# Sigmoid-gated halves of 8192 x 8192: 64 neighbouring rows for each partition

## The chip, the core and the metric

The kernel runs on one core of one Trainium2 chip. The core has compute engines that run side by side: ScalarE (ACT) for functions such as the sigmoid, VectorE (DVE) for elementwise arithmetic, and others that this kernel leaves idle. Data comes from the chip's main memory (HBM, "dram" in names) to the on-chip memory of 128 partitions by DMA transfers. Sixteen DMA engines carry them. A transfer is issued by an engine's queue: here SyncE (SP) issues the loads, ScalarE the stores.

The metric is the device time of a run in microseconds (us).

## The reference

The input x has 8192 rows of 8192 float32 numbers. The left half of each row is multiplied by the sigmoid of the right half:

```python
def reference(x):                       # x: (8192, 8192) float32
    a, b = np.split(x, 2, axis=-1)      # two halves of 4096 columns
    return a * (1 / (1 + np.exp(-b)))   # (8192, 4096) float32
```

The kernel must read 268.4 MB and write 134.2 MB. Each element is used once.

## The kernel before

The rows are cut into 32 tiles of 256 rows. A tile puts two rows on each of the 128 partitions, so a partition holds 2 x 8192 x 4 B = 64 KiB of a tile of x, and 32 KiB of a tile of the result. There are two buffers for x and two for the result, used in turn.

```python
    R = 2
    SLOTS = 2
    n_tiles = n_rows // (P * R)                              # 8192 / 256 = 32
    x_t = x.rearrange("(n p r) m -> n p (r m)", p=P, r=R)    # row = n*256 + p*2 + r
    out_t = out.rearrange("(n p r) m -> n p (r m)", p=P, r=R)

    xs = [pool.tile([P, R * n_cols], fp32, name=f"x_sb{k}") for k in range(SLOTS)]
    os = [pool.tile([P, R * half], fp32, name=f"o_sb{k}") for k in range(SLOTS)]
    ... # (cut)
    for i in range(n_tiles):
        rows = xs[i % SLOTS].rearrange("p (r h m) -> p r h m", r=R, h=2)
        packed = os[i % SLOTS].rearrange("p (r m) -> p r m", r=R)

        load = nc.sync.dma_start(out=xs[i % SLOTS], in_=x_t[i])      # L50
        ... # (cut: waits)
        if 0 < i < n_tiles - 1:
            parts = [(slice(0, R), slice(0, half))]          # one part: the whole tile
        else:
            ... # (cut: first and last tile in four parts)
        def store(cols):
            ins = nc.scalar.dma_start(out=out_t[i, :, cols], in_=os[i % SLOTS][:, cols])   # L62
            ... # (cut)
        for k, (r, c) in enumerate(parts):
            b = rows[:, r, 1, c]
            sig = nc.scalar.activation(out=b, in_=b, func=SIG)                             # L68
            mul = nc.vector.tensor_mul(out=packed[:, r, c], in0=rows[:, r, 0, c], in1=b)   # L69
            ... # (cut: waits; the last tile stores each part)
        store(chunks[-1] if i == n_tiles - 1 else slice(0, R * half))
```

Line numbers after # are those that the profile gives. `x_t[i]` is tile i of the rearranged input: for each partition p it names one run of memory. The load into a buffer waits until the multiply has read the tile that was there. The code that is cut declares which waits are needed, issues the first load early and orders the end of the program.

Of the kernel before, what the change touches and what calls it, by code (L numbers as in the profile page):

```python
# [1 line left out]

# [4 lines left out]


def _tiles(ctx, tc, x, out):

    nc = tc.nc
    P = nc.NUM_PARTITIONS  # L20
    DEP = mybir.DependencyInfo(mybir.DependencyClass.Sync, mybir.DependencyReason.DATA)
    fp32 = mybir.dt.float32
    SIG = mybir.ActivationFunctionType.Sigmoid

    n_rows, n_cols = x.shape
    half = n_cols // 2
    R = 2
    SLOTS = 2
    n_tiles = n_rows // (P * R)
    x_t = x.rearrange("(n p r) m -> n p (r m)", p=P, r=R)  # L30
    out_t = out.rearrange("(n p r) m -> n p (r m)", p=P, r=R)

    pool = ctx.enter_context(tc.tile_pool(name="io", bufs=1))
    xs = [pool.tile([P, R * n_cols], fp32, name=f"x_sb{k}") for k in range(SLOTS)]
    os = [pool.tile([P, R * half], fp32, name=f"o_sb{k}") for k in range(SLOTS)]

    def implied(later, *earlier):
        for e in earlier:
            tc.declare_no_dep(later.ins, e.ins, reason="follows from the waits that are kept")

    gone = [{k: [] for k in ("loads", "sigs", "muls", "stores")} for _ in range(SLOTS)]
    last_stores = [[] for _ in range(SLOTS)]
    for i in range(n_tiles):
        old = gone[i % SLOTS]
        freed = last_stores[i % SLOTS]
        now = {k: [] for k in old}
# [4 lines that stand above are left out]
        implied(load, *old["loads"], *old["sigs"])  # L51
        now["loads"].append(load)

        if 0 < i < n_tiles - 1:
            parts = [(slice(0, R), slice(0, half))]
        else:
            w = half // 2
            parts = [
                (slice(r, r + 1), slice(c * w, (c + 1) * w)) for r in range(R) for c in range(2)
            ]  # L60
        def store(cols):
            ins = nc.scalar.dma_start(out=out_t[i, :, cols], in_=os[i % SLOTS][:, cols])  # L62
            now["stores"].append(ins)

        chunks = []
# [4 lines that stand above are left out]
            implied(sig, *old["sigs"], *old["muls"], *old["loads"])  # L70
            implied(mul, *old["muls"], *old["loads"], *now["loads"])
            by_sigmoid = i % 2 == 1 and len(parts) == 1
            implied(mul, *(s for s in old["stores"] if by_sigmoid or s not in freed))
            if by_sigmoid:
                for s in freed:
                    tc.add_manual_dep(sig.ins, s.ins.name, DEP, reason="frees the output slot")
            tc.keep_in_program_order(sig)
            now["sigs"].append(sig)
            now["muls"].append(mul)
            chunks.append(slice(r.start * half + c.start, r.start * half + c.stop))  # L80
            if i == n_tiles - 1 and k > 0:
                store(chunks[k - 1])
        store(chunks[-1] if i == n_tiles - 1 else slice(0, R * half))
        for s in now["stores"]:
            implied(s, *old["loads"], *old["sigs"], *old["muls"], *now["loads"], *now["sigs"])
        for k in old:
            old[k] += now[k]
        last_stores[i % SLOTS] = now["stores"]


def _launch_early(nc):

    SP = mybir.EngineType.SP
    entry, body = (b.instructions for b in nc.main_func.blocks[:2])
    load = next(i for i in body if i.engine == SP and i.opcode == "DMACopy")
    assert not load.sync_info.on_wait
    body.remove(load)
    where = next(k for k, i in enumerate(entry) if i.engine == SP and i.opcode == "Drain")  # L100
    entry.insert(where, load)


def _close_on_sync(nc):

    SP, POOL = mybir.EngineType.SP, mybir.EngineType.Pool  # L110
    ACT = mybir.EngineType.Activation
    block = nc.main_func.blocks[2].instructions
    waits = block[0]
    assert waits.engine == SP and waits.opcode == "Drain" and len(waits.sync_info.on_wait) > 1
    pool = [i for i in block if i.engine == POOL]
    drain1, gather1, release1, reset, clear, drain2, gather2, release2 = pool
    assert reset.is_reset_sema and clear.opcode == "ISA"
    others = [i for i in block[1:] if i.engine != POOL]
    arrive = [i for i in others[: len(others) // 2] if i.opcode == "Drain"]
    assert len(arrive) == 4  # L120
    body = nc.main_func.blocks[1].instructions
    last = [i for i in body if i.engine == ACT and i.opcode == "DMACopy"][-1].sync_info.on_update[0].id
    final = [w for w in waits.sync_info.on_wait if w.id == last]
    assert len(final) == 1

    def event(engine, wait, update=()):
        return mybir.InstEventSemaphore(
            name=nc.get_next_instruction_name(),
            engine=engine,
            debug=waits.debug,  # L130
            sync_info=mybir.SyncInfo(on_wait=[wait], on_update=list(update)),
        )

    n = len(block)
    for lo, hi in ((reset.reset_range_start, last), (last + 1, reset.reset_range_stop)):
        if lo < hi:
            nc.gpsimd.sem_clear(range(lo, hi))
    clears = block[n:]
    assert clears and all(i.opcode == "ISA" for i in clears)
    back = mybir.SyncUpdate(  # L140
        sync_type="semaphore",
        id=last,
        ant_name=final[0].ant_name,
        update_mode="sem-sub-imm",
        update_value=final[0].wait_value,
        update_reg=None,
    )
    block[:] = [
        *arrive,
        drain1,  # L150
        gather1,
        *(event(POOL, w) for w in waits.sync_info.on_wait if w.id != last),
        reset,
        *clears,
        drain2,
        event(SP, final[0], [back]),
    ]


@with_exitstack  # L160
def kernel(
    ctx: ExitStack,
    tc: tile.TileContext,
    x: bass.AP,
    out: bass.AP,
):
    nc = tc.nc
    with ExitStack() as pools:
        _tiles(pools, tc, x, out)
    tc.close()  # L170
    tc.compile()
    _launch_early(nc)
    _close_on_sync(nc)


# [1 line left out]
_INS = ['x']  # L177
_OUTS = [((8192, 4096), 'float32')]


# [23 lines left out]
```

## Time and profile before

| What | Before |
|---|---|
| Time, median of 3 runs | 933.17 us (933.12 to 933.89) |
| Span of the profiled run | 931.7 us |
| VectorE busy | 278.7 us in 38 multiplies |
| ScalarE busy | 227.1 us, 225.8 of it in 38 sigmoids |
| Read from HBM, written to HBM | 268.44 MB, 134.22 MB |
| Mean rate of all transfers | 432 GB/s |
| Load of one tile, issue to landing (median) | 42.2 us |
| Store of one whole tile, issue to landing (median) | 34.7 us |

"Busy" is the time in which an engine executes an instruction; idle time of an engine that is not the bottleneck costs nothing. For the DMA engines the profile gives the mean busy share of the 16 and the bytes that they moved. A transfer is cut into packets, and the profile counts these, their bytes and their time for each queue: q1 carries the loads, q10 the stores. "Issue to landing" has in it the time in which a transfer stands in its queue behind others. The chain of waits goes back from the last instruction of the run, each time to what released it.

### The profile page before, as it was taken

To read this page: it belongs to the slowest core of one execution; us is meant where nothing else is said; L and a number is where in the kernel's file an instruction comes from. 1 tells how busy PE (TensorE), PEld (TensorE's weight loads), DVE (VectorE), ACT (ScalarE), POOL (GpSimd) and SP (SyncE) were. 2 spreads that over 40 slices of the span, in tenths; PEclk is the share of its full clock that TensorE was granted. 3 is DMA by queue.
4 is the path that set the end of the run, shared out by engine and by line. 5 is a ranking of instruction groups with operands and counts; after the bars stand their busy time and mean duration, and the time that the engine had idled before them with its cause. 6 is when DMAs were issued, how large, how long until landed. Compare 5 with 4: busy or idle time off the path is not lost.

```text
span 931.7 us, 247 instructions
## 1 busy us (share of the span) xinstructions
DVE 278.7 (30%) x38; ACT 227.1 (24%) x39; POOL 0.2 (0%) x4
## 2 busy tenths in 40 slices
DVE  0333213333133331233312333123331233312333
ACT  1323330233311333113331133311333113332033
POOL 0000000000000000000000000000000000000000
DMA  9999999999999999999999999999999999999999
GB/s 405 428 450 428 422 456 405 450 428 428 450 418 438 428 436 442 428 428 450 447 408 428 442 459 428 413 460 411 450 428 425 453 408 447 428 428 450 425 430 405
DMA packets 9649, 402.67 MB, mean 432 GB/s; under 512 B 1072, under 2 KB 1072, under 8 KB 1072
## 3 DMA queue, kind: packets, MB, share of 16 engines
q1 hardware_dynamic: 4608, 268.44, 66.6%
q10 hardware_dynamic: 5040, 134.22, 33.4%
q14 instruction: 1, 0.01, 0.0%
HBM read 268.44 MB, written 134.22 MB: 432 GB/s over the span
## 4 chain that ended last, share of the span: by engine, by line
DMA 73%; DVE 15%; ACT 12%; issue 0%; ACTq 0%
DMA x_sb<-in_x_dram 73%; DVE o_sb L69 15%; ACT x_sb L68 12%; ACTq L62 0%; ACTq L68 0%
## 5 line engine op out<-in xcount | busy, mean ns | idle before, releaser
L69 DVE TENSOR_TENSOR o_sb<-x_sb 128x8192 f32<-128x8192 f32 (+1 forms) x38 | 278.7, 7344 | 647.1 <-ACT x_sb L68 647.1
L68 ACT ACTIVATE x_sb<-x_sb 128x8192 f32<-128x8192 f32 (+1 forms) x38 | 225.8, 5952 | 695.6 <-DMA x_sb<-in_x_dram 694.4
L68 ACT ACT_TABLE_LOAD x1 | 1.3, 1283 | 0.8 <-PEq L188 0.8
L188 POOL MEMSET const-bfloat16-1.0<- 128x1 bf16 x1 | 0.1, 102 | 0.0
L188 POOL MEMSET const-uint8-127<- 128x1 uint8 x1 | 0.1, 102 | 0.0
L188 POOL MEMSET const-float32-0.0<- 128x1 f32 x1 | 0.1, 99 | 0.2 <-issue 0.2
L188 POOL MEMSET const-float32-1.0<- 128x1 f32 x1 | 0.1, 99 | 0.0
## 6 DMA issues: line engine op xcount, KB each, us to landing
out_dram<-o_sb ACTq DMA_DIRECT2D x31, 4096.0 KB, 34.7
out_dram<-o_sb ACTq DMA_DIRECT2D x4, 1024.0 KB, 5.6
x_sb<-in_x_dram SPq DMA_DIRECT2D x32, 42.2
```

Of the source, the lines that this page charges most:

```text
L68: sig = nc.scalar.activation(out=b, in_=b, func=SIG)
L69: mul = nc.vector.tensor_mul(out=packed[:, r, c], in0=rows[:, r, 0, c], in1=b)
L188: nc = _bacc.Bacc("TRN2", target_bir_lowering=False, num_devices=1)
```

## The change

The rows are given to partitions in another order. Before, tile n is a block of 256 neighbouring rows, of which partition p takes rows 2p and 2p+1. After, partition p takes rows 64p to 64p+63 over the whole run, two for each tile: tile n has rows 64p + 2n and 64p + 2n + 1 for every p. Each row is still handled once, and the result of a row goes to the same place in the output as before, as the output is rearranged in the same way. The change is meant to let each partition walk through one region of memory from the first tile to the last.

```diff
@@ -27,8 +27,8 @@
     R = 2
     SLOTS = 2
     n_tiles = n_rows // (P * R)
-    x_t = x.rearrange("(n p r) m -> n p (r m)", p=P, r=R)
-    out_t = out.rearrange("(n p r) m -> n p (r m)", p=P, r=R)
+    x_t = x.rearrange("(p n r) m -> n p (r m)", p=P, r=R)
+    out_t = out.rearrange("(p n r) m -> n p (r m)", p=P, r=R)
```

This is the whole diff. From one partition to the next, a tile of x now steps 64 rows (2 MiB) in memory instead of 2 rows (64 KiB), and a tile of the output 64 rows of 16 KiB (1 MiB) instead of 32 KiB.

## The prediction

> **What bounds the kernel now.** I read the share of busy time first, then the slices, the DMA queues, the chain, the groups by form, and one table of windows. The share of busy time says which engines cannot be the bound:
>
> ```profile
> DVE 278.7 (30%) x38; ACT 227.1 (24%) x39; POOL 0.2 (0%) x4
> ...
> DMA  9999999999999999999999999999999999999999
> ...
> DMA packets 9649, 402.67 MB, mean 432 GB/s; under 512 B 1072, under 2 KB 1072, under 8 KB 1072
> ```
>
> VectorE works 30% of the span, ScalarE 24%, and the 16 DMA engines are at nine tenths or more in all 40 slices. So the transfers bound the kernel. A finer look, at whole periods of two tiles, removes the rounding:
>
> ```profile
> 100.00:158.00 58.00, 17.39 (x2) 14.06 (x2) 0.00 (x0) 1.00 1.00 434
> 390.00:448.00 58.00, 17.38 (x2) 14.06 (x2) 0.00 (x0) 1.00 1.00 434
> 738.00:796.00 58.00, 17.39 (x2) 14.06 (x2) 0.00 (x0) 1.00 1.00 434
> ```
>
> The columns are the stretch and its length, then VectorE, ScalarE and GpSimd busy, the clock, the DMA share and GB/s. Early, in the middle and late, the share is 1.00 and the rate 434 GB/s: there is no gap in which a transfer waits for an engine. The queues split that time:
>
> ```profile
> q1 hardware_dynamic: 4608, 268.44, 66.6%
> q10 hardware_dynamic: 5040, 134.22, 33.4%
> ```
>
> q1 is the loads (268.44 MB = 8192 x 8192 x 4 B), q10 the stores. 268.44 MB in 66.6% of 16 x 931.7 us is 27.0 GB/s for one DMA engine, and 134.22 MB in 33.4% is 27.0 GB/s too: a load and a store cost the same per byte now. The counts of packets tell their sizes: 32 loads x 128 partitions = 4096 pieces of 64 KiB, plus 32 x 16 = 512 small ones, is 4608. The small ones I take to be the completion signals (one for each engine and transfer: 67 transfers x 16 = 1072, as the page counts under 512 B).
>
> ```profile
> L69 DVE TENSOR_TENSOR o_sb<-x_sb 128x8192 f32<-128x8192 f32 x30 | 260.8, 8692 | 608.1 <-ACT x_sb L68 608.1
> L68 ACT ACTIVATE x_sb<-x_sb 128x8192 f32<-128x8192 f32 x30 | 210.9, 7031 | 652.8 <-DMA x_sb<-in_x_dram 652.8
> ...
> DMA x_sb<-in_x_dram 73%; DVE o_sb L69 15%; ACT x_sb L68 12%; ACTq L62 0%; ACTq L68 0%
> ```
>
> The chain gives 27% to ScalarE and VectorE, which looks like a gain to be had there. It isn't: the chain goes through one buffer slot, 42 us of load, 7.03 of sigmoid and 8.69 of multiply, and while the 15.7 us of compute run, the other slot's load and a store hold the DMA engines full, as the 1.00 says. ScalarE idles 652.8 us, all of it for loads.
>
> **What the skill says.** Three places of the Trainium skill bear on this.
> - DMA: Bandwidth & Descriptors, "Where 436 GB/s comes from": the 16 ports of the on-chip memory carry 435.2 GB/s. The trace agrees: 434 measured.
> - HBM Reference, "Specifications (TRN2)": a pair of cores shares about 716 GB/s. If so, memory now has room to spare, and some loss there could stay hidden. No view of this trace shows a memory limit.
> - DMA: Bandwidth & Descriptors, "Latency and other measured facts", the row on row pitch at large powers of two: memory-to-memory copies of 128 partitions x 16 KiB ran at 214 GB/s per direction when the pitch from partition to partition was padded, at 207 with a pitch of 512 KiB, at 164 with 2 MiB, and at 103 with 4 or 8 MiB; the page calls aliasing of memory channels among partitions that run in step an inference. The trace of the kernel before is at a pitch of 64 KiB and is at full rate; it neither shows nor refutes the row.
>
> **The change part by part.** Only two address patterns change.
> - *Engines and waits:* nothing. The order of instructions on each engine is the same: 34 rows on VectorE, 71 on ScalarE, 34 on SyncE in both. The 38 sigmoids and 38 multiplies keep their shapes, so 278.7 and 225.8 us stay.
> - *Pieces:* nothing. A partition still takes two neighbouring rows per tile: 2 x 8192 x 4 B = 64 KiB in one run for the load, 2 x 4096 x 4 B = 32 KiB for the store. The 4608 and 5040 packets stay. That a partition's next tile lies just behind its last one joins no pieces, since each tile is a transfer of its own. I see no saving in it.
> - *Pitch between partitions:* before, 64 KiB in x and 32 KiB in out, so a tile is one block of 8 MiB or 4 MiB. After, 64 rows x 32 KiB = 2 MiB in x, and 64 x 16 KiB = 1 MiB in out. All 128 pieces of a load have the same low 21 bits of address relative to the start of x, and in the trace all 16 engines are busy all the time on pieces of the same size. That is the situation of the row on pitch.
>
> The sum if the row holds in full: at 434 GB/s a load of 8.389 MB is 19.33 us of all the engines and a store of 4.194 MB is 9.66, together 28.99 us per tile; times 32 that is 928 us, and 933.17 less 928 leaves 5 us for ramp, tail and launch. A pitch of 2 MiB has 164/214 = 0.766 of the full rate: the load takes 19.33/0.766 = 25.2 us. For the store at 1 MiB I take halfway between 207 and 164, 185.5/214 = 0.867: 11.1 us. Per tile 36.3 us, times 32 is 1162, plus 5: about 1167 us, 25% slower. This is an estimate from that page, and all of it lies on the path, as the DMA engines have no idle time in which to hide it. Compute, 15.7 us per tile, stays beside it.
>
> I choose to take only part of this. The row was measured with runs of 16 KiB, between memory and memory. Here a run is 64 KiB, at 27.0 GB/s 2.4 us long, and engines that are a few hundred ns apart are at places many KiB apart. One that is held up falls behind, away from the others' addresses, which could loosen the collision. And one side is on-chip memory, not a second pitched tensor. If half of the 234 us comes, the time is 933 + 117 = 1050. Weighed with the chance of no loss at all, I say 1025 us. No rival gives just this number: it lies between the two lumps.
>
> **The rivals.**
> 1. *The ports stay the bound: 930 to 940 us.* The traffic, the pieces and the engines' work are unchanged, the ports are the measured limit at 434, and memory may have reserve. For it: the dead flat rate early, middle and late. Against it: the pitch row, whose 2 MiB case gives 328 GB/s in both directions together, under the 434 needed here. I give this 37%.
> 2. *A partial loss: 955 to 1120 us,* loads slower and stores hardly, with the reasons above. About 40%.
> 3. *The row in full or more: 1120 us and up.* 1167 as worked out; if loads fell to the rate of its worst case, 103/214, a load would take 40.2 us, a tile 51.3 and the run about 1650. That was seen only from 4 MiB up, and so gets little. About 22% in all.
> 4. *Faster.* 402.65 MB at the ports' 435.2 GB/s is 925 us before any ramp, so at most about 0.9% is to be had. Over 2% (under 914.5 us) would take a rate of 440 GB/s: 1%.
>
> A wait that takes the place of the one removed doesn't come into it: no wait is removed. Nor does an engine become the bound: VectorE would have to go from 17.4 us in 58 to all of it.
>
> **Range and chances.** The lower end, 928, is the port floor with a little ramp; the upper, 1200, takes in the row in full with some to spare. Faster 0.01, same 0.37, slower 0.62.
>
> **What would show each step right or wrong.** The packets must still be 4608 and 5040, and the sigmoid and multiply 7031 and 8692 ns; anything else breaks the "nothing" steps. The number to look at is GB/s in a window of 58 us with the DMA share at 1.00: 434 means rival 1, about 346 the row in full. A share still near 1.00 with a lower rate means slower packets, not waits. The split of time between the queues tells which pitch hurts: if loads suffer more than stores, q1's share rises above 66.6% (in full: 25.2/36.3 = 69%). Time from issue to landing of a load, 42.2 us now, should grow with the period of a tile. ScalarE's wait for loads should take up nearly all the added time. The prediction fails if the rate stays at 434, if stores lose more than loads, or if only some of the 16 engines slow down, so that the mean DMA share falls and the end of a load waits for the slowest.

## The result, and the profile after

| | Before | After |
|---|---|---|
| Time, median | 933.43 us | 997.07 us |
| Lowest and highest | 933.12, 934.15 | 987.86, 1016.34 |
| Ratio to before | | 1.064 (95% interval 1.061 to 1.067) |

The change costs 6.4%. The ratio leaves out runs more than 1.5% above the fastest of the same kernel (two of the seven here, and two of the four in e1 below), so by the ratio the change costs 60 us here and 70 in e1, where the medians of all runs say 64 and 82. The runs also spread more than before: 28 us from the lowest to the highest in place of 1. The profile is of a run at the upper end, with a span of 1015.0 us, so its 83 us over the 931.7 of before are more than the 64 us between the medians; shares and places are to be read from it, not the exact size. These are the lines of the page that answer to those shown of before:

```profile
DVE 278.6 (27%) x38; ACT 227.0 (22%) x39; POOL 0.2 (0%) x4
...
DMA  9999999999999999999999999999999999999996
GB/s 356 344 323 378 387 384 430 403 420 421 421 413 433 418 418 431 416 416 411 418 408 412 404 384 403 398 389 398 408 387 402 384 402 394 393 396 400 395 394 278
DMA packets 9649, 402.67 MB, mean 397 GB/s; under 512 B 1072, under 2 KB 1072, under 8 KB 1072
...
q1 hardware_dynamic: 4608, 268.44, 68.3%
q10 hardware_dynamic: 5040, 134.22, 30.8%
...
DMA out_dram<-o_sb 42%; DMA x_sb<-in_x_dram 25%; DVE o_sb L69 15%; ACT x_sb L68 12%; ACTq L62 0%; ACTq L68 0%
```

The engines' work is the same, and so are the 4608 and 5040 packets. The DMA engines are still busy in nearly every slice, but move 397 GB/s on average. A share of busy time times the span is the mean time of one DMA engine: for the loads 0.683 x 1015.0 = 693.2 us, before 0.666 x 931.7 = 620.5; for the stores 312.6 us, before 311.2. What is left of the span, time in which an engine carries neither, is 9.2 us, before 0. So of the 83.3 us, 72.7 are slower loads, 1.4 slower stores and 9.2 idle time; the slice at the very end, at 6 tenths, shows most of that. The shares are rounded to a tenth of a per cent, so each of these times is good to about 1 us.

The same windows as before, with the GB/s in the last column:

```profile
100.00:158.00 58.00, 17.38 (x2) 8.25 (x2) 0.00 (x0) 1.00 1.00 390
390.00:448.00 58.00, 17.38 (x2) 14.06 (x2) 0.00 (x0) 1.00 1.00 424
738.00:796.00 58.00, 17.39 (x2) 14.06 (x2) 0.00 (x0) 1.00 1.01 399
```

With the share at 1.00 a lower rate means that each packet takes longer (by the times of q1, a load packet 2.71 us in place of 2.42); no time is lost in which a transfer waits for a compute engine. But the loss isn't even: 323 to 387 GB/s in the first six slices, above 410 in most of the middle, and near 395 at the end. That course became a question for the experiments.

The waits of ScalarE name a second thing (columns: us in total, times, longest). First before, then after:

```profile
ACT x_sb L68 <- DMA x_sb<-in_x_dram: 694.4, 32, 22.3
```

```profile
ACT x_sb L68 <- DMA x_sb<-in_x_dram: 553.5, 23, 28.0
ACT x_sb L68 <- DMA out_dram<-o_sb: 221.7, 9, 25.8
```

Before, all of this wait was for loads. Now the waits of nine sigmoids are put down to a store. In every second tile the sigmoid waits for its load and for the store that frees the output buffer; before, that store landed 34.7 us after its issue, well ahead of the load's 42.2, and now it takes 46.1 beside 46.8 (the last column, medians):

```profile
out_dram<-o_sb ACTq DMA_DIRECT2D x31, 4096.0 KB, 46.1
...
x_sb<-in_x_dram SPq DMA_DIRECT2D x32, 46.8
```

The engines have come apart. A transfer lands with the last of its 16 completion signals, taken as one for each engine. In the trace before, the first and the last signal of a transfer are at most 1.0 us apart; in the trace after, 12.5 us in the median and up to 15.6. The times to landing of the loads (lowest, median, highest) spread with that. First before, then after:

```profile
DMA to landing us min/median/max: 21.9/42.2/44.0
```

```profile
DMA to landing us min/median/max: 26.4/46.8/58.3
```

The waits for stores are thus a sign of uneven engines, not a cost of their own beside the slow loads: the DMA engines stay busy through them.

### The profile page after: what moved, and what is told of

Its sections match the earlier page's. It is cut to its first block, busy times and chain, and to the rows that moved or that the text cites. A ratio compares the mean times of both kernels' runs of the same rounds, so it can differ in the third digit from the quotient of the medians.

```text
span 1015.0 us, 247 instructions
## 1 busy us (share of the span) xinstructions
DVE 278.6 (27%) x38; ACT 227.0 (22%) x39; POOL 0.2 (0%) x4
## 3 DMA queue, kind: packets, MB, share of 16 engines
q1 hardware_dynamic: 4608, 268.44, 68.3%
q10 hardware_dynamic: 5040, 134.22, 30.8%
## 4 chain that ended last, share of the span: by engine, by line
DMA 66%; DVE 15%; ACT 12%; another core or an unknown queue 6%; ACTq 0%; issue 0%
DMA out_dram<-o_sb 42%; DMA x_sb<-in_x_dram 25%; DVE o_sb L69 15%; ACT x_sb L68 12%; ACTq L62 0%; ACTq L68 0%
## 6 DMA issues: line engine op xcount, KB each, us to landing
out_dram<-o_sb ACTq DMA_DIRECT2D x31, 4096.0 KB, 46.1
x_sb<-in_x_dram SPq DMA_DIRECT2D x32, 46.8
```

## The experiments

The theory: the 16 DMA engines work in step on pieces that are a large power of two apart, and such pieces meet in the same part of memory and hold each other up. Rivals: the wide spread of a tile costs, whatever the pitch; only one of the two transfers matters; the slow start belongs to the first addresses.

**e1: the changed kernel again.** No edit.

> The changed kernel once more, for a second profile of it. Both theories: about 993 us (985 to 1000), with load packets slower than those of before (q1's share near 68%) and stores at their old cost. Collision theory (pieces that are 2 MiB apart meet in the same part of memory): the first 100 us are the slowest, as all engines start in step. Scatter theory (a tile that is spread over 256 MiB costs more than one block, whatever the pitch): the rate is even from start to end.

Measured: 1015.7 us median (998.1 to 1027.8), above the range that both theories gave; ratio 1.075 (1.068 to 1.082), with this chip's 933.2 for the kernel before. The windows of its profile (span 1026.4 us, again a run at the upper end):

```profile
0.00:100.00 100.00, 17.59 (x5) 16.02 (x7) 0.20 (x4) 1.00 1.00 332
...
200.00:300.00 100.00, 33.28 (x4) 25.72 (x4) 0.00 (x0) 1.00 1.00 424
...
400.00:500.00 100.00, 26.08 (x3) 26.15 (x4) 0.00 (x0) 1.00 1.00 420
...
600.00:700.00 100.00, 30.79 (x4) 21.09 (x3) 0.00 (x0) 1.00 1.00 396
...
800.00:900.00 100.00, 26.07 (x3) 21.09 (x3) 0.00 (x0) 1.00 1.00 390
```

The slow start is there again, against the scatter theory's even rate. The fall after 600 us, which neither theory had, is there again too.

**e2 and e3: one transfer at a time.** e2 changes the first line alone, e3 the second alone.

```diff
-    x_t = x.rearrange("(n p r) m -> n p (r m)", p=P, r=R)
+    x_t = x.rearrange("(p n r) m -> n p (r m)", p=P, r=R)        # e2
-    out_t = out.rearrange("(n p r) m -> n p (r m)", p=P, r=R)
+    out_t = out.rearrange("(p n r) m -> n p (r m)", p=P, r=R)    # e3
```

> Only the loads take the new order; the stores go out tile by tile as before, so rows of the result stand in other places than the reference has them. If the 2 MiB pitch of the loads is the cause: the whole loss, 985 to 1000 us. If the 1 MiB pitch of the stores has a part in it (its writes could slow the reads beside them): clearly less than the whole, 950 to 975 us.

> Only the stores take the new order; rows of the result stand in other places than the reference has them. If the loads' pitch is the cause: 933 to 936 us, 434 GB/s. If stores have a part: 945 to 970 us, with store packets slower or load packets slower beside them.

Measured: e2 966.1 us, ratio 1.036 (1.033 to 1.039); e3 944.8 us, ratio 1.013 (1.011 to 1.015). The queues of e2 (span 964.5 us), then of e3 (942.6):

```profile
q1 hardware_dynamic: 4608, 268.44, 67.1%
q10 hardware_dynamic: 5040, 134.22, 32.3%
```

```profile
q1 hardware_dynamic: 4608, 268.44, 66.5%
q10 hardware_dynamic: 5040, 134.22, 33.2%
```

In e2 the loads take 0.671 x 964.5 = 647.2 us, 26.7 more than before; the stores 311.5, as before; some 6 us are idle time. In e3 the loads take 626.8 us, about 6 more although their addresses are the old ones, and the stores 312.9, about 2 more; 3 us are idle time. So both transfers have a part, the loads the larger one, and moved stores cost mainly by slowing the loads beside them. The two alone cost 32.8 and 11.6 us, 44 in sum; together they cost 64 in the first runs and 82 in e1 (60 and 70 by the ratios). The rest comes only when both are moved.

**e4: a tile as widely spread, but the pitch no power of two.** The stores are edited like the loads.

```diff
-    x_t = x.rearrange("(n p r) m -> n p (r m)", p=P, r=R)
+    main = x[: 62 * P].rearrange("(p n r) m -> n p (r m)", p=P, r=R)
+    rest = x[62 * P :].rearrange("(p r) m -> p (r m)", r=R)
+    x_t = [main[k] for k in range(31)] + [rest]
```

> The result is the reference's. Each partition takes 62 neighbouring rows (31 tiles), and the last tile is one block of 256 rows as before. The pitch is 2 MiB less 64 KiB for loads and 1 MiB less 32 KiB for stores; a tile is as widely spread as in the changed kernel. Collision theory (a power of two in the pitch): back to 933 to 938 us. Scatter theory: as the changed kernel, 980 to 1000 us.

Measured: 933.9 us, ratio 1.0003 (0.9994 to 1.0012). The page's slices and queues:

```profile
DMA  9999999999999999999999999999999999999999
GB/s 405 427 450 427 424 450 408 450 427 426 451 426 429 427 455 422 426 440 455 430 413 453 417 448 430 423 451 416 441 427 426 451 423 431 438 453 413 440 431 388
...
q1 hardware_dynamic: 4608, 268.44, 66.6%
q10 hardware_dynamic: 5040, 134.22, 33.4%
```

The whole loss is gone, the slow start with it, at the same spread, run lengths and packets. The scatter theory falls.

**e5: half the pitch.**

```diff
-    x_t = x.rearrange("(n p r) m -> n p (r m)", p=P, r=R)
+    halves = x.rearrange("(h p n r) m -> h n p (r m)", h=2, p=P, r=R)
+    x_t = [halves[a, k] for a in range(2) for k in range(n_tiles // 2)]      # out alike
```

> The result is the reference's. The run is done as two halves of 4096 rows, in each of which a partition takes 32 neighbouring rows: the pitch is 1 MiB for loads and 512 KiB for stores, half that of the changed kernel. Collision theory with a loss that grows with the pitch, as the skill's row has it: a small loss, 936 to 960 us. A theory in which any power of two is as bad as another: as the changed kernel, 990 to 1020 us.

Measured: 952.7 us, ratio 1.020 (1.016 to 1.024). A pitch of 1 MiB for loads and 512 KiB for stores costs 19 us, one of 2 MiB and 1 MiB 64 to 82. At these two pitches the loss grows with the pitch. The spread of a tile is halved too, but by e4 spread alone costs nothing.

**e6: 4 KiB less pitch.**

```diff
-    x_t = x.rearrange("(n p r) m -> n p (r m)", p=P, r=R)
+    x_t = [bass.AP(tensor=x.tensor, offset=k * R * n_cols,      # pitch 2 MiB - 4 KiB
+                   ap=[[64 * n_cols - 1024, P], [1, R * n_cols]]) for k in range(n_tiles)]
```

> As e2 (stores in the old order), but the loads' pitch is 2 MiB less 4 KiB, so a run no longer begins at the beginning of a row and the result is another. If the collision lies in address bits that 4 KiB per partition already spreads: 933 to 936 us, in place of e2's 966. If it takes a shift of a whole run (64 KiB), as e4 had it: as e2, 955 to 970 us.

Measured: 935.5 us, ratio 1.0022 (1.0014 to 1.0030), where e2 had 1.036. A shift of 4 KiB from partition to partition, a sixteenth of a run, takes away over nine tenths of the loss.

**e7: both spread, one at a power of two.** Loads as in e2, stores as in e4.

> Loads with a pitch of 2 MiB; stores spread as widely as in the changed kernel, but with a pitch of 62 rows (1 MiB less 32 KiB). Rows of the result stand in other places. e2 lost 33 us, e3 12, both together 65 to 80. If the extra comes from both pitches being powers of two: as e2, 962 to 972 us. If it comes from the stores being spread beside colliding loads: 985 to 1015 us.

Measured: 960.2 us, ratio 1.029 (1.027 to 1.031), no more than e2. So what both together cost over their sum needs both pitches at a power of two; spread stores beside loads at such a pitch don't make it.

**e8 and e9: every load starts in step.** In both there is one buffer in place of two; in e9 the loads are moved as well.

```diff
-    SLOTS = 2
+    SLOTS = 1
-    x_t = x.rearrange("(n p r) m -> n p (r m)", p=P, r=R)        # e9 alone
+    x_t = x.rearrange("(p n r) m -> n p (r m)", p=P, r=R)
```

> The kernel before with one buffer for x and one for the result in place of two. Each load then starts on idle or nearly idle DMA engines, all at the same moment. Loads and stores of neighbouring rows: load packets at their old cost but for the first of each tile; the chain of one buffer, 29 us of load beside the last store and 15.7 of compute, gives about 45 us per tile and some 1440 us. It is the control for e9.

> e8 with the loads (alone) at a pitch of 2 MiB; rows of the result stand in other places. In e2 the load packets took 2976 ns in the first 65 us and about 2490 in the later ones. Step theory (engines collide while they run in step and then drift apart): here every load starts in step, so the load packets stay slow through the whole run, near 2900 ns, and the time is 60 to 200 us above e8's. Rival (it is the first tiles' addresses, or a start of the memory, that is slow): only the first tiles are slow, and the time is within 35 us of e8's.

The 2976 and 2490 ns are means of e2's load packets, as the trace records them, by the time at which they start; the 65 us are counted from the trace's first record, 11 us before the span begins. Measured: e8 1545.7 us, e9 1771.1. e8 is 105 us over its expectation: a load lands after 32.6 us, not 29, and 32.6 + 15.7 of compute is 48.3 per tile. Slices and loads' queue of e8, then of e9:

```profile
GB/s 276 266 325 271 203 212 289 325 251 195 231 298 325 230 217 230 298 324 207 227 217 325 305 210 212 249 325 295 190 224 266 325 271 203 203 298 323 227 181 352
...
q1 hardware_dynamic: 4608, 268.44, 42.7%
```

```profile
GB/s 230 245 285 212 178 203 261 282 197 187 193 280 264 187 185 219 285 239 182 186 248 285 205 184 203 263 283 208 188 200 261 283 203 183 210 261 277 177 203 292
...
q1 hardware_dynamic: 4608, 268.44, 44.7%
```

The two rows swing as engines idle between tiles, but the peaks are 325 in e8 and 277 to 292 in e9 from the third slice to the last, with no recovery. The times to landing of the loads, of e8, then of e9:

```profile
DMA to landing us min/median/max: 21.7/32.6/34.9
```

```profile
DMA to landing us min/median/max: 26.5/39.8/41.4
```

The share of q1 gives the packet: 0.447 x 1766.5 us x 16 engines / 4096 = 3084 ns in e9, 2582 ns in e8 and, by the same sum, 2528 in e2. The same loads at the same addresses take 26.7 us more than before where queues never run dry, and 0.447 x 1766.5 - 0.427 x 1548.6 = 128.4 us more than the control where every load starts afresh on all engines. The rival about first addresses falls. The runs differ by more, 225 us, also more than the 60 to 200 expected, as a tile now ends later too: the first and the last completion signal of a transfer are 1.0 us apart in e8's trace and 5.0 in e9's (medians), and the engines idle until the last has come.

Not every slow start comes from the pitch. In e8's trace, with the packets of a load in order of start, the first sixteen, one for each engine, take 3707 ns on average and the rest 2419 to 2430. In e9's the first sixteen take 3724, and each later group of sixteen between 2699 and 3608. So a load on idle engines loses 1.3 us at either pitch; what the pitch of 2 MiB adds lies in the packets behind. That the engines are in step is what their common start makes of them; no view shows it directly.

**e10 and e11: runs of 16 KiB.** In both each load is cut into four; in e11 the loads are moved as in e2.

```diff
-        load = nc.sync.dma_start(out=xs[i % SLOTS], in_=x_t[i])
+        for j in range(4):
+            quarter = slice(j * n_cols // 2, (j + 1) * n_cols // 2)
+            load = nc.sync.dma_start(out=xs[i % SLOTS][:, quarter], in_=x_t[i][:, quarter])
```

> The kernel before with each load cut into four transfers of 16 KiB for each partition. The pitch and the bytes stay. 933 to 940 us: it is the control for e11.

> e10 with the loads (alone) at a pitch of 2 MiB; rows of the result stand in other places. The runs are 16 KiB, those of the skill's row on pitch, where the whole rate fell to 0.77. If the long run of 64 KiB is what let the engines draw apart in e2: clearly more than e2's 966, and at 0.77 for the loads about 1120 us. If the length of a run doesn't matter: 960 to 975 us.

Measured: e10 958.3 us, ratio 1.026 (1.025 to 1.028), over its expectation; e11 1044.1 us, ratio 1.120 (1.116 to 1.123), clearly over e2's 966 but short of 1120. Loads' queue of e10 (span 957.3 us), then of e11 (1042.0):

```profile
q1 hardware_dynamic: 18432, 268.44, 67.0%
```

```profile
q1 hardware_dynamic: 18432, 268.44, 69.4%
```

The pitch costs 86 us here and 33 in e2. The loads run at 0.670 x 957.3 / (0.694 x 1042.0) = 641.4/723.1 = 0.89 of their control's rate, in e2 at 620.5/647.2 = 0.96. So the pitch costs more with the cut loads, but not the loss to 0.77 (164 GB/s against 214) that the Trainium skill has for 2 MiB (DMA: Bandwidth & Descriptors, "Latency and other measured facts"). That was for memory-to-memory copies; for these loads the measurement decides. Cutting a load also keeps all partitions within the same 16 KiB of their runs until a quarter is done, so this pair doesn't part the length of a packet from that.

**e12: where the extra of both comes from.**

```diff
-            ins = nc.scalar.dma_start(out=out_t[i, :, cols], in_=os[i % SLOTS][:, cols])
+            ins = nc.scalar.dma_start(out=out_t[(i + 16) % n_tiles, :, cols], in_=os[i % SLOTS][:, cols])
```

> The changed kernel (both pitches a power of two), but the result of tile i is stored where that of tile i + 16 (mod 32) belongs, half a partition's region (512 KiB) further; rows of the result stand in other places. It asks where the extra of both pitches together comes from. In two profiles of the changed kernel the rate is about 420 GB/s from 200 to 500 us and 390 to 400 from 600 us on. Distance theory (loads and stores also meet each other, and how much depends on the distance between the place read and the place written, which moves by 32 KiB with each tile): the slow and the fast part change places, under 405 GB/s from 200 to 500 us and 415 or more after 600. Drift theory (the extra is the engines' uneven progress, whatever the distance): the same course as in the changed kernel, 415 to 425 in the middle and 390 to 400 after 600 us. The time by either: 980 to 1030 us.

Measured: 1015.6 us, ratio 1.091 (1.084 to 1.097). Its windows:

```profile
200.00:300.00 100.00, 30.36 (x4) 21.09 (x3) 0.00 (x0) 1.00 1.01 410
...
400.00:500.00 100.00, 27.27 (x4) 26.42 (x4) 0.00 (x0) 1.00 1.00 406
...
600.00:700.00 100.00, 26.07 (x3) 21.09 (x3) 0.00 (x0) 1.00 1.00 413
...
800.00:900.00 100.00, 26.08 (x3) 22.78 (x4) 0.00 (x0) 1.00 1.00 395
```

Slow and fast parts didn't change places: the last part, at 395, is still the slowest of these. The distance theory, as put, falls. The middle, at 406 to 413, is under the drift theory's 415 to 425, so that isn't confirmed either. What makes both pitches together cost more than their sum, and why the rate falls late, stays open. One thing goes with the fall in all three traces: it sets in about when the first and the last completion signal of every transfer of a whole tile have come to lie 12 us or more apart, near 500 us in the first profile, 550 in e1 and 700 in e12. In e2 they stay within 12 us, and the rate doesn't fall. That is a coincidence in time and no cause shown.

## Why the prediction was right, and where it wasn't

- *Nothing in engines and pieces:* right. Packets, sigmoids and multiplies are as before.
- *All loss on the path, as slower packets with the DMA share at 1.00:* right for 72.7 of the profile's 83.3 us, the slower loads. One sign of failure came in part: loads do wait for the slowest engine (12.5 us between first and last signal), but the share falls only in the last slice, with 9.2 us of idle time in all.
- *The pitch as the cause:* right in kind, and shown. e4 and e6 take the power of two away and the loss with it, and e5 halves the pitch and loses less.
- *Loads suffer, stores hardly:* right in the queues, 68.3% for q1. But the stores' pitch isn't free: in e3 it slows the loads. The working took the two losses as a sum, and both together cost more than the two alone (64 to 82 us against 44).
- *The size:* 92 us forecast (1025), 64 measured (997), and 82 in e1. The term that was mis-sized is the share of the row on pitch that is kept: "If half of the 234 us comes" was the choice; 64 us are 27% of it. In the working, the loads were to fall to 0.766 of their rate and the stores to 0.867. Measured in the profile after: 620.5/693.2 = 0.895 and 311.2/312.6 = 0.996. Half of the row would be 94 us for the loads and 24 for the stores, where the profile has 72.7 and 1.4; so the step "I take halfway between 207 and 164" for the stores had no counterpart, and the loads' term was too large as well. That 1025 lies near is luck in part: it weighs a half that didn't come with a chance of no loss that didn't come either.
- *Its reasons for taking only a part:* not settled. e10 and e11 agree with a part of the long run, but don't isolate it. e9 agrees with engines that draw apart and lose less, since there each load starts afresh and all stay slow. But engines that are apart aren't safe: late in the changed kernel, 13 us apart, a load packet takes 2.76 us (600 to 700 us of the profile after) against 2.52 between 200 and 300 us. The third reason, that one side is on-chip memory, no run here tests.
- *"ScalarE's wait for loads should take up nearly all the added time":* half right. Its idle time grew by 81 us, but nine of the waits are put down to stores.
- *No number for the spread of the runs:* missed. The changed kernel's time hangs on how the engines happen to lie to each other, or so the step theory would have it; that was not tested by itself.

What is shown is that the pitch causes the loss. That pieces meet in one part of the memory isn't shown by any view here. The word of the Trainium skill's row for it, aliasing of channels, is an inference there and stays one.

## What to carry to other kernels

When partitions read or write at a pitch that is a large power of two, transfers of the same size and number can get slower while the DMA share stays at 1.00: look at GB/s beside the share. Keep a tile one block of memory, or shift the pitch; 4 KiB less for each partition was enough for the loads here. The same pitch cost 3.5% where the queues never ran dry and 15% where every load started afresh (e2 beside before, e9 beside e8).

## What the hardware showed that was not expected

- Stores at a pitch of 1 MiB slow the loads beside them (by about 6 us) more than themselves (about 2 us).
- Loads and stores that both stand at such a pitch cost 64 to 82 us, against 44 for the two alone, and the time of such a kernel varies by up to 30 us from run to run on one chip.
- Loads of neighbouring rows that are cut from 8 MiB into four of 2 MiB took 958 us instead of 934: 641.4 us for the loads instead of 620.5.
- A load issued together with a store on idle engines landed after 32.6 us, where the full rate would give 29.0. By e8's trace 1.0 us passes before the first packet starts, and the first packet of each engine takes 3.71 us in place of 2.42; the other 1.3 us stay open.
